# Where h and the sums of x begin in their rooms, in a four-FFN encoder trunk on one core

## The chip, the core and the metric

The kernel runs on one core of one Trainium2 chip. The metric is the device time of one execution in microseconds (us). The kernel before takes 943.37 us, the median of three runs (941.68 to 945.07).

## The reference

Two layers, each of three blocks with a residual and a layer norm behind each: a SwiGLU FFN, a mixer, and another SwiGLU FFN. The mixer of layer 0 is a bidirectional mLSTM, that of layer 1 a windowed attention with sinks. 256 tokens, width 1024, FFN width 2816, everything in float32.

```python
def swiglu(x, w_in, w_out):
    gu = x @ w_in
    g, u = gu[..., :D_FF], gu[..., D_FF:]
    return (jax.nn.silu(g) * u) @ w_out

for l in range(DEPTH):                                   # DEPTH = 2
    x = layer_norm(ALPHA * x + 0.5 * swiglu(x, ffn_w_in[l, 0], ffn_w_out[l, 0]), ln_g[l, 0], ln_b[l, 0])
    y = mlstm_mixer(x, ...) if l % 2 == 0 else window_attention(x, ...)
    x = layer_norm(ALPHA * x + y, ln_g[l, 1], ln_b[l, 1])
    x = layer_norm(ALPHA * x + 0.5 * swiglu(x, ffn_w_in[l, 1], ffn_w_out[l, 1]), ln_g[l, 2], ln_b[l, 2])
```

## The kernel before

**Three products for one.** TensorE multiplies in fp32r. Each float32 operand is split into a high part (a cast on ScalarE) and a low part (what is left, a subtraction on VectorE), and `mm3` (line 467) issues three matmuls: high by high, high by low, low by high. The first operand of a matmul is the *stationary* block: 128 by 128 words, loaded into the array before the matmul (the profile's PEld rows). The second is the *moving* one: up to 512 columns that stream past it. In the trace a tile name pair such as `pw<-w_hi,S_lo` gives the moving operand first and the stationary one second.

**Who is stationary.** In the FFNs the weights move (w_hi, w_lo, pieces of 512 columns), and the activations are stationary: `xT` (x transposed, 8 blocks of 128 rows by 256 tokens), `h` (the hidden values transposed, in `hT`), and the sums `S1` to `S4`. In the mixers the q, k and gate projections have 256 columns, or have xT moving.

**An FFN** (`ffn`, line 570) runs four times. A first piece of 512 hidden columns is plain. Then come three groups (`GROUPS`), each of a plain unit of 256 columns and a unit done by seven products of half-blocks instead of eight (`seven`, line 719): its stationary operands are xT for three products and S1 to S4 for four. The sums are built once per FFN by `x_raw` and `x_sum` (lines 622 and 625) from `xr`, which adds xT's two parts up again. Between these run the down products (`down`, line 690), whose stationary operand is h. So TensorE's program alternates: some blocks of 12 or 24 matmuls on xT, 12 or 24 on h, 24 on the sums, and so on, and four transposes now and then (`tr`, line 592).

**Order.** The order on each engine is written out by hand in program order (`manual_schedule`); `Paced` (line 48) keeps a rough account of each engine's time, and `Weights.fill` (line 264) places the splits of weights behind matmuls by that account. The account knows sizes and not addresses.

**Rooms.** Tiles are taken from pools, and a tile with a tag rotates among the rooms of that tag. In the pool of an FFN: `h_hi`, `h_lo` (two rooms each of 1024 words in a partition, which `xr` uses too), `hc_hi`, `hc_lo` (one room each of 512 words, for the plain units), the sums (one room of 512 words for each of eight names), the raw weights, and six temporaries. As laid out, a partition has these bytes as begins of rooms: w_hi 35168 and each 4096 further, w_lo 76128 and each 4096 further, xT_hi 125280, xT_lo 133472, h_hi 141920 and 146016, h_lo 150112 and 154208, and the last rooms of the FFN, for the sums and hc, from 203360 in steps of 2048 to 221792. All of these are 32 more than a multiple of 64. In the attention mixer q_hi begins at 176896 and q_lo at 185088, multiples of 64. In the mLSTM mixer v is stored as rows of 258 words for each of four heads.

The lines that give the rooms their shapes:

```python
return tuple(pool.tile([128, width, S], FR, name="h" + e, tag=tag + e, bufs=n_) for e in ("_hi", "_lo"))           # 577
xr = [pool.tile([128, 8, 128], F32, name=f"xr{t}", tag="h" + e, bufs=2) for t, e in enumerate(("_hi", "_lo"))]     # 619
xs[name] = tuple(pool.tile([128, 4, 128], FR, name=name + e, tag=name + e, bufs=1) for e in ("_hi", "_lo"))        # 629
```

Of the kernel before, what the change touches and what calls it, by code (L numbers as in the profile page):

```python
# [9 lines left out]
F32 = mybir.dt.float32  # L10
FR = mybir.dt.float32r
# [5 lines left out]
D = 1024  # L17
S = 256
# [18 lines left out]
PEND = [6, 4, 6, 6, 6]  # L37


AHEAD = 300.0  # L40
SOON = -1000.0
LANDING = 2200.0
# [98 lines left out]
class Weights:  # L141
# [122 lines left out]
    def fill(self):  # L264

        nc = self.nc
        while True:
            act, vec = max(nc.act, nc.pe), max(nc.vec, nc.pe)
            if act < nc.pe + AHEAD and len(self.half) < 2 and self.made < min(self.room, len(self.plan)):
                p = self.plan[self.made]  # L270
                if (p["word"] in self.raw and nc.when(self.raw[p["word"]]) < act + SOON
                        and not any(p["needs"] == x for x in [h[0] for h in self.half] + [s_[0] for s_ in self.sums])):
                    self.high()
                    continue
            if vec < nc.pe + AHEAD:
                if self.half and nc.when(self.half[0][1]) < vec + SOON:
# [38 lines left out]
def trunk_kernel(ctx: ExitStack, tc: tile.TileContext, x, ffn_w_in, ffn_w_out, ln_g, ln_b, ml_w_in, ml_gate_b,  # L315
# [170 lines left out]
    def split_evac(dst, src, scale=None):  # L486
        if scale is None:
            nc.scalar.copy(dst[0], src)
            nc.vector.tensor_sub(dst[1], src, dst[0].bitcast(F32))
        else:  # L490
            nc.scalar.activation(dst[0], src, AF.Copy, scale=scale)
            nc.vector.scalar_tensor_tensor(dst[1], src, scale, dst[0].bitcast(F32), op0=OP.mult, op1=OP.subtract)
# [77 lines left out]
    def ffn(l, i, n, pending, last):  # L570
        with ExitStack() as ph:
            pool = ph.enter_context(tc.tile_pool(name="ffn", bufs=1))
            hT = {}

            def h_room(width):
                tag, n_ = ("h", 2) if width == 4 else ("hc", 1)
                return tuple(pool.tile([128, width, S], FR, name="h" + e, tag=tag + e, bufs=n_) for e in ("_hi", "_lo"))

            def temp(name):
                return pool.tile([128, 512], F32, name=name, tag="t", bufs=6)  # L580
# [35 lines left out]
                nc.vector.tensor_mul(hh, sg, ps)  # L616
                hs.append(hh)

            xr = [pool.tile([128, 8, 128], F32, name=f"xr{t}", tag="h" + e, bufs=2) for t, e in enumerate(("_hi", "_lo"))]
            xs = {}  # L620

            def x_raw(t):
# [2 lines left out]
            def x_sum(name, a, op, b):  # L625

                f = temp(name).rearrange("p (k m) -> p k m", k=4)
                nc.vector.tensor_tensor(f, a, b, op=op)
                xs[name] = tuple(pool.tile([128, 4, 128], FR, name=name + e, tag=name + e, bufs=1) for e in ("_hi", "_lo"))
                split_evac(xs[name], f)  # L630
                return f

# [3 lines left out]
            def x_one():  # L636
                f1["S1"] = x_sum("S1", xr[1][:, low], OP.subtract, xr[1][:, high])

            def x_two():
                f1["S2"] = x_sum("S2", f1["S1"], OP.subtract, xr[0][:, low])  # L640

            def x_rest():
                x_sum("S4", xr[0][:, high], OP.add, f1["S2"])
                x_sum("S3", xr[0][:, low], OP.subtract, xr[1][:, low])

            hB = h_room(4)
            chunks(hB, 4)
            hB0 = hB
# [70 lines left out]
            def seven(full, unit_turn):  # L719

                of = lambda k0, t: (lambda k: pair(xT, A, k0 + k, tok(t)))
                sum_ = lambda name: (lambda k: pair(xs[name], A, k))
                v = {}
                hB = h_room(4)
                chunks(hB, 4)
                qa, qc = wbank(), wbank()
# [47 lines left out]
            for g in range(GROUPS):  # L774
# [15 lines left out]
                for t in range(2):  # L790
                    sg = temp("sg")[:, 0:256]
                    nc.scalar.activation(sg, ps[t][:, 0:256], AF.Silu)
                    hh.append(temp("hh")[:, 0:256])
                    nc.vector.tensor_mul(hh[t], sg, ps[t][:, 256:512])
                hp = h_room(2)
                chunks(hp, 2)
                down(1)
# [518 lines left out]
    for j, (kind, l, i, n) in enumerate(stages):  # L1316
        last = j == len(stages) - 1
        bound[0] = j
        nc.filler = W.fill if kind == "ffn" else None
        if kind == "ffn":  # L1320
            pending = ffn(l, i, n, pending, last)
        elif kind == "mlstm":
            pending = mlstm(l, n, pending, last)
        else:
            pending = attn(l, n, pending, last)
# [29 lines left out]
```

## Time and profile before

| what | value |
|---|---|
| median of three runs | 943.37 us |
| the profiled execution | 943.43 us |
| its span, first to last instruction | 941.7 us |
| mean granted TensorE clock | 0.997 |
| matmuls | 4416 |
| moved from HBM | 185.68 MB read |

PE is TensorE's matmuls, PEld its weight loads, DVE VectorE, ACT ScalarE, POOL GpSimd, SP SyncE. `pw` and `py` are PSUM banks for the up and the down products. Nearly all instructions are recorded under line 132, the helper that issues them, so groups are told apart by the names of their tiles. A group's row gives the count, the busy time, the mean time of one in ns, and the idle time of the engine before it. A matmul's recorded time is longer than its share of TensorE, since the next one starts before it ends; how far two starts lie apart is read from the start times.

### The profile page before, as it was taken

How to read it: one execution, taken by the hardware profiler on the slowest of the kernel's cores; microseconds unless marked ns; L12 is line 12 of the kernel's file. 1: busy time of each engine (PE TensorE's matmuls, PEld its weight loads, DVE VectorE, ACT ScalarE, POOL GpSimd, SP SyncE). 2: the span in 40 equal slices, each digit the busy share in tenths (PEclk: the TensorE clock that was granted, in tenths of full speed). 3: DMA queues.
4: the chain of work that ended last, by engine and by line, in shares of the span. 5: the costliest groups of instructions: out<-in, count | busy, mean ns of one | idle time of the engine just before them, and what ended most of it. 6: DMA issues, size and time to landing. Idle time of an engine off the chain costs nothing.

```text
span 941.7 us, 12338 instructions
## 1 busy us (share of the span) xinstructions
PE 924.8 (98%) x4416; PEld 764.9 (81%) x4416; DVE 799.8 (85%) x943; ACT 547.1 (58%) x781; POOL 102.8 (11%) x162
## 2 busy tenths in 40 slices
PE   8999999999999999999999999999999999999996
PEld 7788888889878778888888888887887788888885
DVE  6899998787697799988888899978878888898975
ACT  5655756347563548565535576563678554757460
POOL 2010101011111000101010101010545300000100
PEclk9999999999999999999999999999999999999998
DMA  8968773646534949685549597746543267869531
GB/s 270 358 168 315 207 271 77 214 134 208 173 110 154 308 144 331 170 326 134 178 155 341 121 331 207 254 88 202 172 143 111 68 210 260 230 217 310 161 88 45
DMA packets 98461, 187.54 MB, mean 199 GB/s; under 512 B 6720, under 2 KB 37456, under 8 KB 98400
## 3 DMA queue, kind: packets, MB, share of 16 engines
q1 hardware_dynamic: 91648, 174.09, 53.9%
q0 software_dynamic: 6752, 12.66, 8.5%
q8 instruction: 35, 0.57, 0.3%
q14 instruction: 26, 0.21, 0.1%
HBM read 185.68 MB, written 1.05 MB: 198 GB/s over the span
## 4 chain that ended last, share of the span: by engine, by line
PE 72%; DVE 12%; DMA 5%; ACT 5%; issue 3%; SPq 1%; POOL 1%; DVEq 0%; ACTq 0%; POOLq 0%
PE pw L132 45%; PE py L132 27%; DVE w_lo L132 5%; DMA s_raw<-in_ffn_w_in_dram 2%; ACT w_hi L132 2%; DMA w_raw<-in_ffn_w_in_dram 1%; DMA w_raw<-in_ffn_w_out_dram 1%; SPq L98 1%; DVE x L132 1%; DMA x<-in_x_dram 1%; ACT sc L132 1%; DVE s_raw L132 1%; DVE h L132 1%; DVE o L132 1%; SPq L96 0%
## 5 line engine op out<-in xcount | busy, mean ns | idle before, releaser
L132 DVE TENSOR_TENSOR w_lo<-w_raw,w_hi 128x1024 fp32r<-128x1024 f32 (+1 forms) x237 | 280.8, 1215 | 19.8 <-ACT w_hi L132 18.1
L132 ACT CAST w_hi<-w_raw 128x1024 fp32r<-128x1024 f32 (+1 forms) x237 | 240.8, 1049 | 79.7 <-DMA w_raw<-in_ffn_w_in_dram 24.0
L132 PE MATMUL pw<-w_hi,xT_hi 128*128 128x512 f32 x560 | 222.4, 397 | 0.3 <-ACT xT_hi L132 0.3
L132 PE MATMUL pw<-w_hi,xT_lo 128*128 128x512 f32 x560 | 218.9, 391 | 0.1
L132 PE MATMUL pw<-w_lo,xT_hi 128*128 128x512 f32 x560 | 218.5, 390 | 0.3 <-DVE w_lo L132 0.2
L132 ACT CAST w_hi<-s_raw 128x1024 fp32r<-128x1024 f32 x144 | 148.4, 1051 | 93.0 <-DVE s_raw L132 57.1
L132 DVE TENSOR_TENSOR w_lo<-s_raw,w_hi 128x1024 fp32r<-128x1024 f32 x144 | 172.5, 1219 | 18.9 <-ACT w_hi L132 18.7
L132 PE MATMUL py<-w_hi,h_hi 128*128 128x512 f32 x352 | 138.2, 393 | 0.3 <-ACT h_hi L132 0.3
L132 PE MATMUL py<-w_hi,h_lo 128*128 128x512 f32 x352 | 137.4, 390 | 0.2 <-DVE h_lo L132 0.2
L132 PE MATMUL py<-w_lo,h_hi 128*128 128x512 f32 x352 | 137.1, 390 | 0.2 <-DVE w_lo L132 0.2
L132 PEld LDWEIGHTS pw<-w_hi,xT_lo 128*128 128x128 f32 x560 | 105.1, 188 | 23.4 <-DVE xT_lo L132 0.9
L132 PEld LDWEIGHTS pw<-w_lo,xT_hi 128*128 128x128 f32 x560 | 105.3, 188 | 21.6 <-DVE w_lo L132 1.1
L132 PEld LDWEIGHTS pw<-w_hi,xT_hi 128*128 128x128 f32 x560 | 105.2, 188 | 20.8 <-ACT xT_hi L132 0.7
L132 DVE TENSOR_TENSOR s_raw<-s_raw 128x1024 f32<-128x1024 f32 x72 | 87.0, 1219 | 0.6
L261 POOL DMA_DIRECT2D s_raw<-in_ffn_w_in_dram x24 | 29.0, 1209 | 498.8 <-DVE w_lo L132 417.0
L132 PEld LDWEIGHTS py<-w_hi,h_lo 128*128 128x128 f32 x352 | 66.1, 188 | 15.2 <-DVE h_lo L132 1.4
L132 PEld LDWEIGHTS py<-w_lo,h_hi 128*128 128x128 f32 x352 | 66.1, 188 | 14.0 <-DVE w_lo L132 0.6
L132 PEld LDWEIGHTS py<-w_hi,h_hi 128*128 128x128 f32 x352 | 66.1, 188 | 13.9 <-ACT h_hi L132 0.7
L132 PE MATMUL pw<-w_hi,S_hi 128*128 128x512 f32 x192 | 74.8, 390 | 0.2 <-ACT e L132 0.2
L132 PE MATMUL pw<-w_hi,S_lo 128*128 128x512 f32 x192 | 74.7, 389 | 0.0
L132 PE MATMUL pw<-w_lo,S_hi 128*128 128x512 f32 x192 | 74.7, 389 | 0.0
L132 DVE TENSOR_TENSOR h_lo<-pw,h_hi 128x512 fp32r<-128x512 f32 x44 | 30.2, 687 | 24.8 <-ACT h_hi L132 24.7
(218 smaller groups left out, 1113.8 us busy)
## 6 DMA issues: line engine op xcount, KB each, us to landing
w_raw<-in_ffn_w_out_dram SPq DMA_DIRECT2D x88, 512.0 KB, 5.4
s_raw<-in_ffn_w_in_dram SPq DMA_DIRECT2D x72, 512.0 KB, 6.0
w_raw<-in_ffn_w_in_dram SPq DMA_DIRECT2D x56, 512.0 KB, 5.1
w_raw<-in_ffn_w_in_dram SPq DMA_DIRECT2D x96, 256.0 KB, 4.5
s_raw<-in_ffn_w_in_dram POOLq DMA_DIRECT2D x24, 512.0 KB, 6.0
w_raw<-in_ml_w_in_dram SPq DMA_DIRECT2D x24, 512.0 KB, 4.9
w_raw<-in_at_w_in_dram SPq DMA_DIRECT2D x12, 512.0 KB, 4.2
w_raw<-in_ml_w_out_dram SPq DMA_DIRECT2D x8, 512.0 KB, 4.0
```

What stands on the lines that cost most here:

```text
L98: self.nc.sync.dma_start(ap, source)
L132: r = f(out, *args, **kw)
L261: nc.gpsimd.dma_start(t.rearrange("p (k f) -> p k f", k=self.words[w]["k"]), v, accum_op=OP.add)
```

## The change

Each room of h grows from its shape to that many words and 32 more (128 bytes), and the tile used is a slice of it that begins `at` words behind the begin of the room. The same is done for the rooms of the sums. FFN number `2 * l + i` takes `H_AT[2 * l + i]` for h and `S_AT[2 * l + i]` for the sums: 1, 2, 3, 4 words and 5, 6, 7, 12 words, that is 4, 8, 12, 16 bytes and 20, 24, 28, 48 bytes. `xr`, which takes turns with h in the same rooms, is given rooms of the same larger size and begins at their begin. xT, the weights and both mixers keep their shapes. No instruction is added or taken away.

```diff
+H_AT = [1, 2, 3, 4]
+S_AT = [5, 6, 7, 12]
...
             def h_room(width):
                 tag, n_ = ("h", 2) if width == 4 else ("hc", 1)
-                return tuple(pool.tile([128, width, S], FR, name="h" + e, tag=tag + e, bufs=n_) for e in ("_hi", "_lo"))
+                return tuple(shifted([width, S], "h" + e, tag + e, n_, H_AT[2 * l + i]) for e in ("_hi", "_lo"))
+
+            def shifted(shape, name, tag, bufs, at):
+
+                n_ = shape[0] * shape[1]
+                t = pool.tile([128, n_ + 32], FR, name=name, tag=tag, bufs=bufs)
+                return t[:, at:at + n_].rearrange("p (k f) -> p k f", k=shape[0])
...
-            xr = [pool.tile([128, 8, 128], F32, name=f"xr{t}", tag="h" + e, bufs=2) for t, e in enumerate(("_hi", "_lo"))]
+            xr = [pool.tile([128, D + 32], F32, name=f"xr{t}", tag="h" + e, bufs=2)[:, 0:D].rearrange("p (k m) -> p k m", k=8)
+                  for t, e in enumerate(("_hi", "_lo"))]
...
-                xs[name] = tuple(pool.tile([128, 4, 128], FR, name=name + e, tag=name + e, bufs=1) for e in ("_hi", "_lo"))
+                xs[name] = tuple(shifted([4, 128], name + e, name + e, 1, S_AT[2 * l + i]) for e in ("_hi", "_lo"))
```

## The prediction

> **What bounds the kernel now.** I read the page from the top: busy shares, then the chain that ended last, then the groups, and last the start times of single matmuls.
>
> ```profile
> span 941.7 us, 12338 instructions
> PE 924.8 (98%) x4416; PEld 764.9 (81%) x4416; DVE 799.8 (85%) x943; ACT 547.1 (58%) x781; POOL 102.8 (11%) x162
> PE 72%; DVE 12%; DMA 5%; ACT 5%; issue 3%; SPq 1%; POOL 1%; DVEq 0%; ACTq 0%; POOLq 0%
> ```
>
> The chain is TensorE for 72% of the span. A busy PE of 98% says little alone, since a matmul's end is modelled and overlaps the next one's start. So I take the chain inside an FFN, which shows whether anything but TensorE is on it, and the engines' busy time in the same stage.
>
> ```profile
> 802.52 2.72 PE py L132 x12
> 805.24 5.44 PE pw L132 x24
> ...
> 770.00:915.00 145.00, 145.00 (x659) 120.00 (x658) 129.82 (x131) 90.06 (x108) 7.25 (x6) 1.00 0.70 221
> ```
>
> The chain there is matmuls alone. The columns are start, length, what, and how many: 12 matmuls of 512 columns take 2.72 us and 24 take 5.44 us, so the **pitch** (from one start to the next) is 226.7 ns. VectorE is busy 129.82 of 145 us and ScalarE 90.06, at a granted clock of 1.00. What an FFN costs is the number of matmuls times their pitch, and each nanosecond of pitch shows in the end.
>
> What is in 226.7 ns? In the mixer the same three-product form runs with 256 columns. The first and the fifth start of such a run:
>
> ```profile
> 219.73 0.28 PE L132 MATMUL pw<-xT_lo,w_hi 128*128 128x256 f32 x1
> ...
> 220.21 0.28 PE L132 MATMUL pw<-xT_hi,w_lo 128*128 128x256 f32 x1
> ```
>
> These are 4 pitches in 0.48 us, 120 ns each. So 256 columns more cost 226.7 - 120 = 106.7 ns, 0.417 ns a column; 512 columns are 213.3 ns, and **13.3 ns belong to each matmul whatever its length**. Every one loads new weights, so 13.3 ns is what the load of a stationary block costs the stream beside it. It is the most that a better distance could give back.
>
> **What the change touches.** These six groups have h or a sum as the stationary operand.
>
> ```profile
> L132 PE MATMUL py<-w_hi,h_hi 128*128 128x512 f32 x352 | 138.2, 393 | 0.3 <-ACT h_hi L132 0.3
> L132 PE MATMUL py<-w_hi,h_lo 128*128 128x512 f32 x352 | 137.4, 390 | 0.2 <-DVE h_lo L132 0.2
> L132 PE MATMUL py<-w_lo,h_hi 128*128 128x512 f32 x352 | 137.1, 390 | 0.2 <-DVE w_lo L132 0.2
> L132 PE MATMUL pw<-w_hi,S_hi 128*128 128x512 f32 x192 | 74.8, 390 | 0.2 <-ACT e L132 0.2
> L132 PE MATMUL pw<-w_hi,S_lo 128*128 128x512 f32 x192 | 74.7, 389 | 0.0
> L132 PE MATMUL pw<-w_lo,S_hi 128*128 128x512 f32 x192 | 74.7, 389 | 0.0
> ```
>
> Together 3 x 352 + 3 x 192 = 1632 matmuls. No instruction is added or removed. What moves is the byte at which a stationary block begins, against the byte at which the moving weights begin. Laid out as the rooms are now, w_hi and w_lo, xT, h and the sums all begin 32 bytes past a multiple of 64, and every block inside them is a multiple of 512 bytes further: the distance is 0 modulo 64 everywhere in the FFNs. Afterwards it is 4, 8, 12, 16 bytes for h and 20, 24, 28, 48 for the sums in the four FFNs. The rooms grow by 128 bytes, so whatever lies behind them keeps its place modulo 64.
>
> **Does the trace show that distance matters?** One stage has another one: in the attention mixer q begins on a multiple of 64, 32 bytes out of step with the weights. Its output projection, in a stretch where TensorE waits for nothing:
>
> ```profile
> L132 PE MATMUL py<-w_hi,q_hi 128*128 128x512 f32 x11 | 4.4, 399 | 0.0
> L132 PE MATMUL py<-w_hi,q_lo 128*128 128x512 f32 x11 | 4.3, 394 | 0.0
> L132 PE MATMUL py<-w_lo,q_hi 128*128 128x512 f32 x11 | 4.3, 392 | 0.0
> ```
>
> The same shape as the sums above and as free of idle time; it takes 399, 394 and 392 ns, the sums 390, 389 and 389. By start times:
>
> ```profile
> 747.57 0.40 PE L132 MATMUL py<-w_hi,q_hi 128*128 128x512 f32 x1
> ...
> 749.67 0.40 PE L132 MATMUL py<-w_hi,q_hi 128*128 128x512 f32 x1
> ```
>
> Nine pitches in 2.10 us, 233.3 ns: **32 bytes out of step cost 6.7 ns a matmul**, half of the load's 13.3 again, and the pattern of three repeats without settling. At distance 0 the pitch is also not 226.7 at once. After a group of transposes:
>
> ```profile
> 415.36 0.40 PE L132 MATMUL pw<-w_lo,xT_hi 128*128 128x512 f32 x1
> ...
> 417.68 0.39 PE L132 MATMUL pw<-w_hi,xT_lo 128*128 128x512 f32 x1
> 417.90 0.39 PE L132 MATMUL py<-w_hi,h_hi 128*128 128x512 f32 x1
> 418.13 0.39 PE L132 MATMUL py<-w_lo,h_hi 128*128 128x512 f32 x1
> ```
>
> Ten pitches in 2.32 us, 232 ns, and only then 220 to 230, that is 226.7: weight load and stream fall into step after some ten matmuls, which cost 10 x 5.3 = 53 ns together. Stepping from xT to h (417.68 to 417.90) costs nothing, because both have distance 0.
>
> **The sum.** (1) The new pitch of h and the sums is the unknown; the trace has no distance under 32 bytes with 512 columns. Its nearest rows are 0 bytes (no loss) and 32 bytes (6.7 ns). An estimate between those two, straight in the distance: h is out by 10 bytes on average, 6.7 x 10/32 = 2.1 ns, times 1056 is 2.2 us; the sums are out by 20, 24, 28 and, 48 being 16 short of 64, by 16: 22 on average, 4.6 ns, times 576 is 2.6 us. Together 4.8 us. If any distance but 0 costs the full 6.7 ns, it is 1632 x 6.7 = 10.9 us; if none costs anything, 0. Below that, up to 13.3 x 1632 = 21.8 us could be won. I take 4.8, since the distances spread evenly between the two rows. (2) Falling into step anew. In an FFN these matmuls come in blocks of 12 and 24 between blocks of xT; the program has 103 places where xT, h and the sums follow each other without a transpose between. At 53 ns each that is 5.5 us at most, 0 at least; I take 2.5 us, about half, since some of the settling shows only its last steps. Sum: 4.8 + 2.5 = **7.3 us**. The profiled execution took 943.43 us for its span of 941.7; the median before is 943.37, the same within 0.1. 943.4 + 7.3 is about **951 us**.
>
> (3) The writers of h and the sums now write to odd words. The mixer's v is written so already, its rows being 258 words, beside h's present rows:
>
> ```profile
> L132 DVE TENSOR_TENSOR h_lo<-pw,h_hi 128x512 fp32r<-128x512 f32 x44 | 30.2, 687 | 24.8 <-ACT h_hi L132 24.7
> L132 ACT CAST h_hi<-pw 128x512 fp32r<-128x512 f32 x44 | 25.7, 584 | 29.9 <-PE pw L132 29.9
> L132 DVE TENSOR_TENSOR v_lo<-pw,v_hi 128x512 fp32r<-128x512 f32 x4 | 2.7, 682 | 0.0
> L132 ACT CAST v_hi<-pw 128x512 fp32r<-128x512 f32 x4 | 2.3, 586 | 0.4 <-PE pw L132 0.4
> ```
>
> 682 against 687 and 586 against 584 ns: nothing. Were a write 10% slower, 44 x 69 ns = 3 us would go to VectorE, which has 15 us of slack in a stage of 145 us; it is hidden.
>
> **Rivals.** *Faster: the distance takes the load's reads out of the stream's way.* Price: any part of 13.3 ns. The least, median and longest time of one, over all of a group that is in and out of step:
>
> ```profile
> L132 PE MATMUL py<-w_hi,h_hi x352: 387/389/500, 43.6 to 933.4; 128*128 128x512 f32 x176
> ```
>
> The shortest is 2 ns under the median; 2 x 1632 is 3.3 us, 940.1 us; the whole 13.3 gives 921.6. VectorE's slack of 10% would carry it. It decides where h's pitch falls under 226. Against it, the mixer's value products move v with rows at 8, 16 and 24 bytes out of step. Head 0 (0 or 32 bytes out), then head 1 (24):
>
> ```profile
> L132 PE MATMUL py<-v_hi,a_hi 128*128 128x258 f32 x6 | 1.7, 285 | 0.0
> L132 PE MATMUL py<-v_hi,a_lo 128*128 128x258 f32 x6 | 1.7, 285 | 0.0
> L132 PE MATMUL py<-v_lo,a_hi 128*128 128x258 f32 x6 | 1.7, 283 | 0.0
> ```
>
> ```profile
> L132 PE MATMUL py<-v_hi,a_hi 128*128 128x258 f32 x6 | 1.7, 284 | 0.0
> L132 PE MATMUL py<-v_hi,a_lo 128*128 128x258 f32 x6 | 1.7, 283 | 0.0
> L132 PE MATMUL py<-v_lo,a_hi 128*128 128x258 f32 x6 | 1.7, 282 | 0.0
> ```
>
> 1 to 2 ns better than 32 bytes out of step, not 13: no distance there frees the stream. That is short runs of another length, so the chance is 22%.
>
> *No change: what costs 13.3 ns is not where the block lies,* and the output projection is slow for another reason than its 32 bytes (its place after a mixer, its tile). Then the time is 943.4. 14%. [...]
>
> *Much slower: a block that doesn't begin on four words costs more reads.* 4 words for h and 12 for the sums, in the last FFN, would be spared; three quarters of 1632, 1224 matmuls, would pay. If the load's cost doubled, 1224 x 13.3 = 16.3 us, 959.7 us. 14%. No row here has a full stationary block at such a place. [...]
>
> **Chances.** 50% for the forecast (its own range 946.5 to 957), 22%, 14% and 14% for the rivals in that order. What a measurement of this kernel can tell from no change is about 0.3%, 2.8 us. Faster by more than that: the first rival but for small gains, 22%. Within: the second rival, 14%. Slower: 50 + 14 = 64%. The range reaches from 938, where half of the faster rival is left out (11%), to 960, which leaves out the far end of the last one (6%).
>
> **What would show it.** Right: in FFN stages, h and S groups with a mean near 391 to 396 ns and not 389, different from FFN to FFN and worst in the sums of FFN 2 and 3; xT groups a little up after each h block; VectorE idle more. The chain rows of 12 matmuls would read 2.75 to 2.80 us. Wrong: rows of 2.72 us still (second rival), or below 2.71 us (first), or the means of 402 (third). If one FFN gains and another loses, the sum by distance fails though the mechanism holds.

## The result, and the profile after

The kernel after takes 947.56 us (median of four runs, 946.64 to 948.98) against 942.92 us before (four runs, 941.68 to 945.07): the two medians are 4.6 us apart. The ratio on record, which is not simply that of the two medians, is 1.006 with an interval of 1.0046 to 1.0073. The forecast was 951, its own range 946.5 to 957. The profiled execution took 946.64 us with a span of 944.8, at a granted clock of 0.998. Below are the busy shares and xT's groups, then those whose stationary operand is h or a sum.

```profile
PE 929.2 (98%) x4416; PEld 765.9 (81%) x4416; DVE 801.0 (85%) x943; ACT 547.8 (58%) x781; POOL 103.1 (11%) x162
...
L134 PE MATMUL pw<-w_hi,xT_hi 128*128 128x512 f32 x560 | 222.5, 397 | 0.2 <-ACT xT_hi L134 0.2
L134 PE MATMUL pw<-w_hi,xT_lo 128*128 128x512 f32 x560 | 218.9, 391 | 0.0
L134 PE MATMUL pw<-w_lo,xT_hi 128*128 128x512 f32 x560 | 218.3, 390 | 0.0
L134 PE MATMUL py<-w_hi,h_hi 128*128 128x512 f32 x352 | 139.2, 395 | 0.3 <-ACT h_hi L134 0.3
L134 PE MATMUL py<-w_hi,h_lo 128*128 128x512 f32 x352 | 138.4, 393 | 0.0
L134 PE MATMUL py<-w_lo,h_hi 128*128 128x512 f32 x352 | 138.4, 393 | 0.6 <-DVE w_lo L134 0.6
L134 PE MATMUL pw<-w_lo,S_hi 128*128 128x512 f32 x192 | 75.3, 392 | 0.0
L134 PE MATMUL pw<-w_hi,S_lo 128*128 128x512 f32 x192 | 75.2, 392 | 0.0
L134 PE MATMUL pw<-w_hi,S_hi 128*128 128x512 f32 x192 | 75.2, 392 | 0.0
```

Set these against the same groups of before. h: 139.2 + 138.4 + 138.4 = 416.0 us against 138.2 + 137.4 + 137.1 = 412.7, so 3.3 us more. The sums: 225.7 against 224.2, 1.5 us more. Together 4.8 us, about the 4.6 between the medians. The first xT group has 222.5 us now, the other two 218.9 and 218.3: no loss there that this view can tell.

The chain in the second FFN reads, with start, length, what and how many:

```profile
385.57 5.54 PE py L134 x24
391.11 5.91 PE pw L134 x28
397.02 2.77 PE py L134 x12
```

Twelve matmuls on h take 2.77 us where they took 2.72, and 24 take 5.54 where they took 5.44: the pitch is 231 ns and not 226.7. In this stretch nothing else has come onto the chain.

For the rest I use the pitch itself: the difference of the start times of two consecutive matmuls, over all whose stationary operand is h (or a sum) and which have 512 columns. Differences of 260 ns and more are left out: there TensorE waited, or had just run transposes (some 315 ns behind each group of them, before and after alike). The *excess* is the sum of what each pitch has above 226.67 ns.

| | FFN 1 | FFN 2 | FFN 3 | FFN 4 | excess, us |
|---|---|---|---|---|---|
| h before, ns | 227.4 | 227.2 | 227.2 | 227.1 | 0.57 |
| h after | 230.6 | 231.9 | 230.6 | 228.8 | 3.90 |
| sums before | 226.7 | 226.7 | 226.8 | 226.7 | 0.02 |
| sums after | 230.8 | 231.4 | 226.8 | 229.8 | 1.74 |
| xT before, all FFNs | | | | | 1.98 |
| xT after, all FFNs | | | | | 2.15 |

Pitch on h and the sums gained 3.33 + 1.72 = 5.05 us, xT 0.17. The two spans differ by 3.1 us only, because the profiled execution of before had 2 us more of differences over 260 ns (all 512-column matmuls on xT, h and the sums). The median differs by 4.6.

### The profile page after: what moved, and what is told of

It is laid out like the page before. It is cut to its first block, busy times and chain, and to the rows that moved or that the text cites. A ratio compares the mean times of both kernels' runs of the same rounds, so it can differ in the third digit from the quotient of the medians.

```text
span 944.8 us, 12338 instructions
## 1 busy us (share of the span) xinstructions
PE 929.2 (98%) x4416; PEld 765.9 (81%) x4416; DVE 801.0 (85%) x943; ACT 547.8 (58%) x781; POOL 103.1 (11%) x162
## 4 chain that ended last, share of the span: by engine, by line
PE 80%; DVE 9%; ACT 4%; DMA 3%; issue 2%; POOL 1%; SPq 0%; DVEq 0%; ACTq 0%; POOLq 0%
PE pw L134 52%; PE py L134 29%; DVE w_lo L134 4%; DMA w_raw<-in_ffn_w_in_dram 2%; ACT w_hi L134 1%; ACT sc L134 1%; DVE h L134 1%; DMA w_raw<-in_ffn_w_out_dram 1%; DVE o L134 1%; DMA w_raw<-in_ml_w_in_dram 0%; DVE x L134 0%; DVE rm L134 0%; ACT o L134 0%; DVE s_raw L134 0%; ACT xT_hi L134 0%
## 5 line engine op out<-in xcount | busy, mean ns | idle before, releaser
L134 PE MATMUL pw<-w_hi,xT_hi 128*128 128x512 f32 x560 | 222.5, 397 | 0.2 <-ACT xT_hi L134 0.2
L134 PE MATMUL pw<-w_hi,xT_lo 128*128 128x512 f32 x560 | 218.9, 391 | 0.0
L134 PE MATMUL pw<-w_lo,xT_hi 128*128 128x512 f32 x560 | 218.3, 390 | 0.0
L134 PE MATMUL py<-w_hi,h_hi 128*128 128x512 f32 x352 | 139.2, 395 | 0.3 <-ACT h_hi L134 0.3
L134 PE MATMUL py<-w_lo,h_hi 128*128 128x512 f32 x352 | 138.4, 393 | 0.6 <-DVE w_lo L134 0.6
L134 PE MATMUL py<-w_hi,h_lo 128*128 128x512 f32 x352 | 138.4, 393 | 0.0
```

What stands on the lines that cost most here:

```text
L134: r = f(out, *args, **kw)
```

## The experiments

My theory was the prediction's: the stationary block begins at some distance from the moving weights, and the load then falls out of step with the stream. The rivals were that the room's growth alone does it, that an odd begin does it, and that the distance counts modulo something other than 64. Ratios are against the kernel before on the same chip.

**Rooms only.** The change with every tile at the begin of its longer room.

```diff
-H_AT = [1, 2, 3, 4]
-S_AT = [5, 6, 7, 12]
+H_AT = [0, 0, 0, 0]
+S_AT = [0, 0, 0, 0]
```

> The rooms grow by 32 words as in the change, but h and the sums begin at the begin of their rooms (all offsets 0). If the distance between the begins of weights and stationary block modulo 64 bytes decides (theory D): h and the sums are back at a pitch of 226.7 ns (recorded time 389 ns), excess over 226.7 under 0.7 us in all, time as before within 0.3%. If the place of the rooms modulo 256 bytes decides, which the growth by 128 bytes changes (theory R): h in the rooms that are now 128 bytes out stays above 228 ns, 1 to 4 us over before. If the begin of a block off a multiple of four words decides (theory B): as before.

Measured: 947.47 us, 1.0059 (1.0039 to 1.0078). The words of H_AT and S_AT aren't needed for the loss; 128 bytes more in a room are enough. Its chain, again in the second FFN:

```profile
348.72 2.80 PE py L134 x12
351.52 5.57 PE pw L134 x24
...
385.53 5.44 PE py L134 x24
390.97 5.91 PE pw L134 x28
```

The block at 385.53 is as fast as before, the one at 348.72 is at 233 ns. The fast one reads an h_hi room at 141920 and an h_lo room at 150368; the slow one reads rooms that lie 128 bytes further, modulo 256, than the weights do (146144 and 154592). The weights and xT begin 96 past a multiple of 256 (35168 is 137 x 256 + 96). So 128 is not the same as 0, as it would be modulo 64. The distance counts modulo something above 128. (Which room a block reads is worked out from the order of the rooms in the kernel; the pitch agrees: in all four FFNs the chunks of h that fall in the second room are at 231.8 to 233.2 ns, and those in the first, among other blocks, at 226.7.)

**h only and the sums only.** From the change, `S_AT = [0, 0, 0, 0]` in the one and `H_AT = [0, 0, 0, 0]` in the other.

> h begins 1, 2, 3, 4 words late, the sums at the begin of their rooms. Theory D and theory B: h keeps the pitches of the change (230.6, 231.9, 230.6, 228.8 ns in the four FFNs, 3.9 us over 226.7), the sums fall back to 226.7; 945 to 947 us. If blocks out of step throw the next ones out (knock-on): the sums stay at 228 or more behind h, about 1 us more.

> The sums begin 5, 6, 7, 12 words late, h at the begin of its rooms. Theory D: the sums keep 230.8, 231.4, 226.8, 229.8 ns (1.7 us over 226.7), h falls back to 227.2 (0.6 us); 944 to 946 us. Knock-on: h stays above 228. Theory B: the same as D, but FFN 3 with its 7 words has no place in it.

Measured: 947.4 (1.0058, 1.0039 to 1.0077) and 947.7 (1.0058, 1.0039 to 1.0077). Undoing half of the change gave nothing back, in either half. The excess says why: with the sums at offset 0 theirs is 2.80 us, with h at offset 0 its own is 4.15, since the long rooms alone put half of them 128 bytes out. These two were built on the wrong modulus and don't separate h from the sums.

They do show something else: what stands before a block counts too. In the third FFN of the kernel with the sums only, the sums begin 28 bytes behind the begins of the same rooms in each of the three groups. In the first group they stand behind blocks of h that are 128 bytes out, in the second behind blocks of h that are in step:

```profile
529.93 2.79 PE py L134 x12
532.72 5.61 PE pw L134 x24
...
578.20 2.72 PE py L134 x12
580.91 5.44 PE pw L134 x24
```

The same 24 matmuls on the same two sums take 5.61 us behind a slow block and 5.44 behind one in step.

**Rooms of 256 bytes more, without and with the words.** If the period is 256, this growth moves nothing.

```diff
-                t = pool.tile([128, n_ + 32], FR, name=name, tag=tag, bufs=bufs)
+                t = pool.tile([128, n_ + 64], FR, name=name, tag=tag, bufs=bufs)
...
-            xr = [pool.tile([128, D + 32], F32, ...
+            xr = [pool.tile([128, D + 64], F32, ...
```

> As the run with the rooms alone, but they grow by 64 words (256 bytes) and not by 32; offsets 0. Theory R (the place modulo 256 bytes decides, and the growth by 128 bytes was the loss): h and the sums are back at 226.7 ns, under 0.7 us over it in all, time as before within 0.3%. If any growth of the rooms costs (where the tiles lie, waits between stages): again 0.5% slower.

> The change's own offsets (1, 2, 3, 4 and 5, 6, 7, 12 words) in rooms that grow by 256 bytes, so that the distances modulo 256 are exactly 4, 8, 12, 16 and 20, 24, 28, 48 bytes in every room. If the few words cost by themselves (the forecast): h 2 ns and the sums 4.6 ns over 226.7, about 5 us, 947 to 949 us. If only the 128-byte growth cost: 226.7 ns, time as before. If the words cost less the nearer they are to 0: h of the first FFN near 227 and the sums of FFN 2 and 3 worst.

Measured, without the words: 941.56 us, 0.9996 (0.9987 to 1.0005), the time of before. With the change's words: 947.55, 1.0052 (1.0035 to 1.0069). The chain of the first in the second FFN:

```profile
381.90 5.44 PE py L134 x24
387.34 5.91 PE pw L134 x28
393.25 2.72 PE py L134 x12
395.96 5.44 PE pw L134 x24
```

All these blocks are back at 226.7 ns. The four ratios side by side:

| ratio to before | rooms +0 or +256 bytes | rooms +128 bytes |
|---|---|---|
| offset 0 | 0.9996 | 1.0059 |
| the change's offsets | 1.0052 | 1.0060 |

The two losses don't add, because they are one cause: the longer rooms and the words both move the distance. In the kernel of the change half of h's blocks are out by 128 bytes and the words together, and that can be better than either alone. The same 24 matmuls on h in the first FFN, 4 bytes out (words alone), 128 bytes out (rooms alone), and 132 bytes out (the change):

```profile
140.93 5.57 PE py L134 x24
140.30 5.59 PE py L134 x24
140.79 5.44 PE py L134 x24
```

At 132 bytes they are in step. The blocks in the same place are at about 233 ns in FFN 2 and 3 of the change (136 and 140 bytes) and at 226.7 in FFN 4 (144 bytes). With 256 bytes of growth each FFN has one clean distance. The high sums in FFN 1 to 4 (20, 24, 28 and 48 bytes out):

```profile
L134 PE MATMUL pw<-w_hi,S_hi 128*128 128x512 f32 x48 | 18.9, 395 | 0.0
L134 PE MATMUL pw<-w_hi,S_hi 128*128 128x512 f32 x48 | 18.9, 394 | 0.0
L134 PE MATMUL pw<-w_hi,S_hi 128*128 128x512 f32 x48 | 18.7, 389 | 0.0
L134 PE MATMUL pw<-w_hi,S_hi 128*128 128x512 f32 x48 | 19.0, 396 | 0.0
```

28 bytes out is as fast as 0 here. The mean pitches, beside the straight line that the prediction drew between 0 and 32 bytes:

| bytes out | 4 | 8 | 12 | 16 | 20 | 24 | 28 | 48 |
|---|---|---|---|---|---|---|---|---|
| operand | h | h | h | h | sums | sums | sums | sums |
| line, ns above 226.7 | 0.8 | 1.7 | 2.5 | 3.3 | 4.2 | 5.0 | 5.9 | 3.3 |
| measured, ns above | 5.5 | 4.1 | 1.1 | 0.9 | 6.5 | 3.9 | 0.0 | 6.4 |

Of h's excess 0.4 to 0.7 ns are there at distance 0 too, from the end of each FFN, so at 12 and 16 bytes most of h's blocks are in step.

**Steps of 64 bytes.** Rooms of 256 bytes more, and 16, 32, 48, 64 words in FFN 1 to 4 for both h and the sums.

> Rooms grown by 256 bytes; h and the sums begin 64, 128, 192 and 256 bytes late in FFN 1, 2, 3, 4. Theory D (distance modulo 64): all 226.7 ns. Theory R: 226.7 in FFN 4 alone, 232 to 234 in FFN 2 (as the rooms 128 bytes out in the run with the rooms alone), and FFN 1 and 3 between 228 and 236.

Measured: 947.63 us in its one run. The high sums by FFN:

```profile
L134 PE MATMUL pw<-w_hi,S_hi 128*128 128x512 f32 x48 | 19.0, 396 | 0.0
L134 PE MATMUL pw<-w_hi,S_hi 128*128 128x512 f32 x48 | 18.9, 394 | 0.0
L134 PE MATMUL pw<-w_hi,S_hi 128*128 128x512 f32 x48 | 18.8, 392 | 0.0
L134 PE MATMUL pw<-w_hi,S_hi 128*128 128x512 f32 x48 | 18.7, 389 | 0.0
```

In pitches 233.3, 232.7, 228.9 and 226.7 ns at 64, 128, 192 and 256 bytes; h has 233.3, 232.6, 229.0 and 227.1. The whole loss at 64, none at 256: the place counts modulo 256 bytes. In all these runs the weights begin 96 behind a multiple of 256, and only the stationary blocks moved.

**The words exchanged.** 256 bytes more; h 5, 6, 7, 8 words, the sums 1, 2, 3, 4. It asks whether the operand or the distance sets the pitch.

> Rooms grown by 256 bytes; now h stands at 20, 24, 28, 32 bytes and the sums at 4, 8, 12, 16 in FFN 1 to 4, the other way round than in the run with the change's own offsets. If the distance alone sets the pitch: h about 233.2, 230.6, 227 (with its settling), and 230 to 234 at 32; the sums about 232, 230.8, 227.8, 227.6. If it belongs to h or to the sums, to the FFN or to the place of the block in the program: h keeps 232, 231, 228, 227.6 by FFN.

Measured: 948.22 us in its one run. The sums at 4, 8, 12 and 16 bytes have 232.7, 230.8, 226.7 and 233.2 ns; h at 20, 24, 28 and 32 has 233.0, 230.9, 228.7 and 233.1. Of the seven distances under 64 bytes that both operands have had, five agree within 1.2 ns. At 28 bytes h has 228.7 and the sums 226.7 (next experiment); at 16 bytes h had 227.6 above, and the sums have 233.2 here. So the distance alone doesn't settle the pitch at every place.

**All at 28 bytes, all at 64 bytes.** 256 bytes more; `[7, 7, 7, 7]` for both lists, then `[16, 16, 16, 16]`.

> Rooms grown by 256 bytes, h and the sums 7 words (28 bytes) late in all four FFNs. If 28 bytes is a distance that falls into step like 0: sums 226.7 and h 227.2, time as before within 0.3%, though every block begins off four words. Linear in the distance, as forecast: 6.7 x 28/32 = 5.9 ns on 1632 matmuls, 9.6 us, 952 us. A begin off four words: 3 us or more.

> Rooms grown by 256 bytes, h and the sums 16 words (64 bytes) late in all four FFNs, where one FFN showed 233.3 ns. By the pitch: 6.6 ns on 1632 matmuls, 10.7 us less the 0.5 us of settling that h has now; 951.5 to 953.5 us. If TensorE's waits give a part back: 948 to 951.

Measured: 944.72 us, 1.003 (1.0018 to 1.0042), and 951.74, 1.011 (1.0093 to 1.0127). In the first, the sums of FFN 2 to 4 stand at 226.67 ns, and h's down products that lie among other blocks too. The end of each FFN, where the last chunks of h follow one another, does not. Two stretches of the second FFN of this kernel, the chain among other blocks and a group at the end, from 470.8 to 481.6 us:

```profile
395.78 2.72 PE py L134 x12
398.50 5.44 PE pw L134 x24
```

```profile
L134 PE MATMUL py<-w_lo,h_hi 128*128 128x512 f32 x14 | 5.5, 395 | 0.0
```

Same tile, same distance; 2.72 us for twelve in one place of the program, 395 ns (389 is in step) in the other. The stretch at the end begins behind a wait and four transposes, out of step. The kernel before has the same stretch, begins it out of step too (its first pitches are 224 to 236 ns, as the prediction saw behind transposes) and is at 226.7 after ten matmuls. At 28 bytes it never gets there. One group in the same 4 us, from 474.8 to 478.8, before and here:

```profile
L132 PE MATMUL py<-w_lo,h_hi 128*128 128x512 f32 x6 | 2.3, 389 | 0.0
L134 PE MATMUL py<-w_lo,h_hi 128*128 128x512 f32 x7 | 2.8, 395 | 0.0
```

Here the pitches go 231, 236, 231, 236 to the end of the stretch, and the first block of xT behind it, at distance 0, is back at 226.7 within ten matmuls. So in this kernel, at 28 bytes, a stream that is in step stays in step and one that is out stays out; at 0 one that is out comes back. It isn't so behind every slow block: in the kernel of the change the sums of FFN 3 are in step (226.8) right behind blocks of h that are 140 bytes out, at 233 ns. With all at 64 bytes every block is out, whatever stands before it:

```profile
386.40 5.60 PE py L134 x24
...
397.96 2.80 PE py L134 x12
400.76 5.60 PE pw L134 x24
```

The blocks of h and the sums are at 233.3 ns on average. The pitches gained 6.34 + 3.82 = 10.2 us there and xT 0.7, 10.9 together; the medians differ by 9.9.

**All operands one word on.** w_hi, w_lo and xT as well as h and the sums begin one word into their rooms; this was meant to leave every distance and make the begins odd. The rooms of w_hi, w_lo and xT grew by 64 bytes for it, and a scratch tile shares another tile's room to make place.

```diff
-        hi = self.pool.tile([128, D], FR, name="w_hi", tag="w_hi", bufs=RING)
+        hi = self.pool.tile([128, D + 16], FR, name="w_hi", tag="w_hi", bufs=RING)[:, 1:D + 1]
...
-H_AT = [1, 2, 3, 4]
-S_AT = [5, 6, 7, 12]
+H_AT = [1, 1, 1, 1]
+S_AT = [1, 1, 1, 1]
```

> Weights, xT, h and the sums all begin one word behind the begin of their rooms: each begins off a multiple of four words, and all distances in the FFNs are 0 modulo 64 again. Theory D: 226.7 ns for xT, h and the sums in the FFNs, time as before within 0.5% (the attention's output projection then is at another distance, under 1 us either way). Theory B (a begin off four words costs reads): xT, h and sums all at 229 to 233 ns, 8 us or more over before.

Measured: 969.22 us, 1.0287 (1.0268 to 1.0306), by far the slowest. But a room that is 64 bytes longer puts each further room of w 64 bytes on, so this was no test of odd begins alone. The control is the kernel before with only those longer rooms of w_hi and w_lo, its tiles at their begin:

> The kernel before with only the rooms of w_hi and w_lo grown by 64 bytes, so that the weights begin at 0, 64, 128 or 192 bytes against xT, h and the sums, changing from piece to piece; nothing begins off four words. If the distance explains the run with everything one word late: the same 235 to 237 ns in xT, h and the sums, 965 to 970 us. If the odd word of the weights did it: 226.7 to 233.3 mixed, mean 230 to 232, 955 to 962 us.

Measured: 954.08 us in its one run. Pitches are 231.6 ns on xT, 231.8 on h, 231.4 on the sums; in the kernel that is one word on they are 236.6, 236.4 and 235.8. The group of xT's high parts, first in the control, then one word on:

```profile
L132 PE MATMUL pw<-w_hi,xT_hi 128*128 128x512 f32 x560 | 224.8, 401 | 0.0
```

```profile
L134 PE MATMUL pw<-w_hi,xT_hi 128*128 128x512 f32 x560 | 227.1, 406 | 0.0
```

Both are above the 397 of before. In the control no stationary block moved modulo 256 (the longer rooms shift what lies behind them by 20 x 64 = 1280 bytes, 5 x 256, worked out from the kernel), so the place of the weights counts as well as that of the stationary block. That only the difference of the two counts is not shown: no run moved both alike and nothing else. Longer rooms of w cost some 12 us; about 15 more, 4.4 to 5.0 ns a matmul, come with the odd word and the rooms of xT, h and the sums that grew beside it. An odd begin of the sums alone need not cost anything (seven words in, with all at 28 bytes, those of FFN 2 to 4 stand at 226.67 ns), which points to the moving operand's begin, but no run moved the weights alone by a word.

**q in step.** The kernel before, with 96 bytes taken ahead of all tiles of the attention mixer, so that q's distance becomes 0 modulo 256 (it was 160).

```diff
+            tile_([128, 24], F32, "ahead")
```

> The kernel before, with the attention mixer's rooms moved 96 bytes up, so that q, k and the weights begin at the same place modulo 256 bytes. Theory R: the output projection goes from 233.3 ns to 226.7 after it has settled, recorded times 399, 394 and 392 ns to 389; some 100 matmuls by 6.7 ns are 0.6 us, too little for the interval. Rival (that stage is slow for another reason): its recorded times stay at 392 to 399.

Measured: 941.71 us, 0.9991 (0.998 to 1.0001). The output projection, in the stretch that the prediction read:

```profile
L132 PE MATMUL py<-w_hi,q_hi 128*128 128x512 f32 x11 | 4.3, 390 | 0.0
L132 PE MATMUL py<-w_lo,q_hi 128*128 128x512 f32 x11 | 4.3, 389 | 0.0
L132 PE MATMUL py<-w_hi,q_lo 128*128 128x512 f32 x11 | 4.3, 389 | 0.0
```

399, 394 and 392 ns have become 390, 389 and 389. This is the row on which the prediction leaned, and it was the place: the mixer and the tile are the same. The whole projection has 96 such matmuls (32 in each of its three groups). Their excess over 226.67 ns goes from 0.55 to 0.23 us, since many stand in short blocks behind waits or transposes and begin out of step with q in its new place too; the time doesn't tell 0.3 us from nothing. No version tried is faster than the kernel before by more than its interval.

## Why the prediction was right, and where it was wrong

**What bounds the kernel: right.** TensorE's pitch is the chain in the FFNs, and what it gained showed in the time: 5.05 + 0.17 us of pitch between the traces, 4.6 in the median. VectorE idles more, as forecast: 944.8 - 801.0 = 143.8 us where it was 941.7 - 799.8 = 141.9.

**Term 1, the pitch of h and the sums: the size right by luck, its reason half wrong.** 4.8 us forecast, 5.05 measured. The mechanism, that the place of the stationary block against the moving one sets the pitch, is shown by the rooms of 256 bytes more (nothing moves modulo 256, and the time is 0.9996 of before) and by q in step (399, 394 and 392 ns become 390, 389 and 389). That the price is paid in the weight load, 13.3 ns of each pitch, stays an estimate from rows of 256 and of 512 columns: every one of the 4416 matmuls has a load, so no row shows a matmul without one. The step that failed is "the distance is 0 modulo 64 everywhere" with "whatever lies behind keeps its place modulo 64": the period is 256 bytes, so the longer rooms alone cost 1.0059, and q's "32 bytes" were 160. The straight line in the distance failed too: 4 bytes cost h 5.5 ns where it gave 0.8, and 28 cost the sums nothing where it gave 5.9. Over the eight distances the errors happen to cancel: the words without the shifted rooms have an excess of 3.03 + 2.42 us, 4.9 above before's 0.59. "Worst in the sums of FFN 2 and 3" follows from that line and is wrong: FFN 3 has the fastest sums of all. And a distance has no one pitch: what stands before the block counts, for which the prediction had no term within h and the sums.

**Term 2, falling into step anew: mis-sized.** 2.5 us forecast, 0.17 measured on xT. The 53 ns came from a start behind four transposes, and the term charged half of them at all 103 places. But xT follows h or a sum at only 27 of them; at the other 76 the next block is h or a sum. With every block of h and the sums out of step (all at 64 bytes) xT loses 34 ns behind each of the 27, where it lost 5 before: 0.8 us. In the change, where some of these blocks are in step, it loses 10 ns, 0.15 us. What h and the sums lose in their own first matmuls is in term 1's mean. This term, 2.3 us too large, is most of what lies between the sum of 7.3 us and the 4.6 measured.

**Term 3, the writers: right.** In the change h_lo's subtraction and h_hi's cast stay as they were (before 687 and 584):

```profile
L134 DVE TENSOR_TENSOR h_lo<-pw,h_hi 128x512 fp32r<-128x512 f32 x44 | 30.2, 688 | 23.8 <-ACT h_hi L134 23.6
L134 ACT CAST h_hi<-pw 128x512 fp32r<-128x512 f32 x44 | 25.7, 586 | 34.6 <-PE pw L134 34.6
```

**The rivals.** *Faster* falls: none of the distances read cleanly (multiples of 4 bytes up to 32, then 48, 64, 128, 192 and 256) has a mean pitch under 226.66 ns, so the 13.3 ns that the prediction put down to a load are not given back by place. *No change* falls too: the same tiles have 233.3 ns at 64 bytes and 226.7 at 256. *A begin off four words costs more reads* was a supposition of the prediction, with no row of before behind it; it falls for the stationary operand: seven words in, the sums of FFN 2 to 4 stand at 226.67 ns. Whether an odd begin of the moving weights costs time is open.

**Still open:** why 12, 28, 132 and 144 bytes hold the step and the distances beside them don't; why 16 was in step for h and not for the sums; whether only the difference of the two begins counts; and what in the chip has the period of 256 bytes. The runs show where the step is lost, not what loses it.

## What to carry to other kernels

Where each matmul has a weight load of its own, as all 4416 do here, look at where the stationary and the moving tiles begin, modulo 256 bytes, as soon as groups of the same shape differ by 3 to 9 ns in their means (q's 392 to 399 and the sums' 389 and 390 in the kernel before). On the rooms of h and the sums a pad of 256 bytes was free (0.9996) and one of 128 was not (1.0059), nor was one of 64 on the rooms of the weights (954.08 us against 941.82), since these moved the further rooms modulo 256. A distance seen in one row is a residue modulo an unknown period: compute it from the full addresses, and try two periods, before drawing a line through two points. Undoing half of a change tells little where something that both halves share, here the longer rooms, is enough to put the blocks out of step. And when a group is slow, look at the block before it: it may only carry on what that one began, as the sums did that took 5.61 us behind a slow block and 5.44 behind one in step.

## What the runs showed of the hardware

- With the moving weights 96 bytes behind a multiple of 256, the mean pitch of a 512-column fp32r matmul with its own weight load changed with the stationary block's distance from them modulo 256 bytes. Sums: 226.7 ns at 0 (kernel before), 233.3 at 64, 232.7 at 128, 228.9 at 192 and 226.7 at 256 (steps of 64 bytes). Between 0 and 64 it isn't in order: 232.2 for h at 4 and, for the sums, 226.7 at 12 (the words exchanged), 233.2 at 20 and 226.7 at 28 (256 bytes more, the change's words). Nor is it in order above 128: in the third group of each FFN of the kernel of the change, 24 matmuls on h are in step at 226.7 ns 132 and 144 bytes out, and at 233.0 and 233.1 ns 136 and 140 bytes out; with the rooms only, chunks of h that are 128 bytes out are at 231.8 to 233.2.
- It changed with what stood before, too. Sums 28 bytes into their rooms take 5.44 us for 24 behind an h block in step and 5.61 behind one that is out (the sums only). With all at 28 bytes, h has 2.72 us for twelve in one stretch and, behind transposes, 395 ns each, about 233 to 235 from start to start, in another. At 0, in the kernel before, such a stretch is back at 226.7 ns after ten matmuls.
- With the moving operand and all others one word on, pitches are 4.4 to 5.0 ns above the 231.4 to 231.8 of the control with longer rooms of w; of what share the word is, the runs don't say.
